# An encoder trunk on one core: the convolution's output product in three split passes, and the end of the token mixer in written order

## The chip, the core and the metric

The kernel runs on one core of a Trainium2 chip. Its time is the time of one execution on the device, in microseconds (us). A profile of one execution shows what each engine did: TensorE (PE, its weight loads PEld), VectorE (DVE), ScalarE (ACT), GpSimd (POOL), SyncE (SP, which issues most DMAs) and the DMA engines. All five run at the same time, each through its own instructions in order, and wait for each other by semaphores.

## What is computed

Two layers over 256 tokens of width 1024, in f32. Each layer is a SwiGLU block, a token mixer, a second SwiGLU block and a gated embedding. The change is in the mixer:

```
u = rms_norm(h)
q, k, v, c, g = split(u @ w_in)
y_attn = window_attention(q, k, v) @ w_attn_out
c_val, c_gate = split(c)
c = depthwise_conv(c_val * sigmoid(c_gate))        # 31 taps, 512 channels
c = silu(layer_norm(c))
y_conv = c @ w_conv_out                            # 512 -> 1024
g_attn, g_conv = split(sigmoid(g))
h = h + (g_attn * y_attn + g_conv * y_conv) @ w_o  # 1024 -> 1024
```

## The kernel before

Activations lie with channels on the 128 partitions and the 256 tokens along the free axis (T = 256), so a matmul has a weight block of 128 x 128 and a moving block of 128 x 256.

**Split products.** Most products are not done in f32. A weight and an activation are each split into a high and a low part of the type fp32r: ACT rounds the value to the high part (a CAST, L106 for weights), DVE subtracts it from the value for the low part (L107). The product is then three passes in TensorE, high x high, high x low, low x high (`mm3`, L322 to L330). Two products of the mixer are done in plain f32 on the raw weights: attn_out (tile `ps_ao`) and conv_out (`ps_co`), both in `products` at L892. The profile shows one plain f32 matmul as two passes.

**Weights.** The class `Weights` holds a list of loads (units, mostly 1 MB) and of prepared weights (specs). `get()` hands out the next weight and, before that, prepares weights up to `LOOK` = 6 ahead (less `rest`); `prep_upto` loads the raw unit into one of `RAW_BUFS` = 4 buffers (tile `raw`, DMAs at L80) and splits it. A raw buffer is free once its weights are split. `raw_spec` marks a weight that is used as it is: it is not split, and its raw buffer is held until TensorE has used it. `limit()` keeps loads from running past held buffers. `later(n, fn)` calls fn at the n-th next `get()`.

**Order.** A planner orders the instructions of each engine by the program's order, priorities and its own estimate of when things are ready. `keep_in_program_order` pins one instruction behind the one traced before it on its engine. `ws.lag` lowers the priority of weight splits. `group(products, evac)` runs a product and postpones the eviction of its result into the next group.

**The mixer's stages.** conv_in makes the convolution's input; its 31 taps a channel block run on DVE (L643) at low priority beside everything until the gates end. Attention: scores, softmax, `attend` (transposes `ps_pt`, copied by ACT to `pTs`), `gather` (`ps_o`). `gates` makes 16 blocks of g (`ps_g`); attention's steps for the second half of the tokens are hung between them by `later`. `squash` is the sigmoid of g on ACT. Then come four attn_out, with the layer norm between them: `ln_by_token` (transposes of y to `ps_yt`, statistics, `yn`) before the second, `ln_by_channel` (transposes back, `ps_yc`, silu on ACT) before the fourth. Then four conv_out; each eviction multiplies by the gate, adds the attention's part and splits the sum into `ym_h` and `ym_l` (L964, L965, `split` at L471). Then `mix_out` (`ps_wo`) with w_o, one double and six single, whose evictions add to x (L983) and split it for the next block.

PSUM has four tiles of one bank (`mm_tile`) and two of two banks (`at_tile`).

Of the kernel before, what the change touches and what calls it, by code (L numbers as in the profile page):

```python
# [31 lines left out]
NREL = 512  # L32
NEG = -1e9
LOOK = 6
RAW_BUFS = 4
BACKGROUND = 800
WEIGHTS_LAG = 100
ATTN = 7
# [7 lines left out]
class Weights:  # L46
# [4 lines left out]
    def __init__(self, tc, raw_pool, w_pool):  # L51
        self.tc, self.nc = tc, tc.nc
        self.raw_pool, self.w_pool = raw_pool, w_pool
        self.units, self.specs = [], []
        self.raw, self.ready, self.held, self.hooks = {}, {}, {}, []
        self.next_load = self.next_prep = self.next_get = 0
        self.rest, self.pin, self.lag, self.parts = 0, None, 0, 1

    def unit(self, k, n, sources):
# [61 lines left out]
    def later(self, n, fn):  # L121

        self.hooks.append((self.next_get + n - 1, fn))

    def finish(self):
        for _, fn in self.hooks:
            fn()
        self.hooks = []

    def get(self):  # L130
        i = self.next_get
        due = [fn for at, fn in self.hooks if at <= i]
        self.hooks = [h for h in self.hooks if h[0] > i]
        for fn in due:
            fn()
        p0 = self.tc.cur_priority
        self.tc.cur_priority = p0 + self.lag
# [7 lines left out]
def encoder_kernel(ctx: ExitStack, tc: tile.TileContext, a: dict, out: bass.AP):  # L145
# [105 lines left out]
    def mix_specs(l):  # L251
        w = a["w_in"][l]
        c0 = QD + 2 * P

        def conv_specs(j, n):
            uv = cols_unit(w, KD, c0 + j * P, n * P)
            ug = cols_unit(w, KD, c0 + CD + j * P, n * P)
            for c in range(n):
                ws.spec(KD, P, [(uv, 0, c * P, 0, P)])
                ws.spec(KD, P, [(ug, 0, c * P, 0, P)])  # L260

        conv_specs(0, 2)
        ukv = cols_unit(w, KD, QD, 256)
        for i in range(2):
            ws.spec(KC, 256, [(ukv, i * KC, 0, 0, 256)])
        for i in range(2):
            uq = cols_unit(w[i * KC * P : (i + 1) * KC * P], KC, 0, QD)
            for k in range(0, KC, 2):
                ws.spec(2, QD, [(uq, k, 0, 0, QD)])
        conv_specs(2, 2)  # L270
        g0 = QD + 2 * P + 2 * CD
        for j in range(8):
            u = cols_unit(w, KD, g0 + j * 256, 256)
            for c in range(2):
# [44 lines left out]
        return par[:, c0 + l * n + k : c0 + l * n + k + 1]  # L319


    def mm3(ps, w, x, first=True, last=True, k0=0, x_k0=0, n_k=None, cols=slice(0, P)):  # L322
        (wh, wl), (xh, xl) = w, x
        n_k = wh.shape[1] if n_k is None else n_k
        for k in range(n_k):
            kx = x_k0 + k
            f, e = first and k == 0, last and k == n_k - 1
            nc.tensor.matmul(ps, wh[:, k0 + k, cols], xh[:, kx, :], start=f, stop=False)  # L328
            nc.tensor.matmul(ps, wh[:, k0 + k, cols], xl[:, kx, :], start=False, stop=False)  # L329
            nc.tensor.matmul(ps, wl[:, k0 + k, cols], xh[:, kx, :], start=False, stop=e)  # L330

    def by_pass(ps, w, x, n_k):

# [136 lines left out]

    def split(dst, src, c=None):  # L471
        hi, lo = dst
        nc.scalar.copy(out=hi, in_=src)
        nc.vector.tensor_tensor(out=lo, in0=src, in1=hi.bitcast(F32), op=ALU.subtract)


    x_first = x_cur = new_x("xa", "x0")
# [146 lines left out]
    def mix(l, u, st, xn, stat):  # L624
        cw, kg, bias, sink = (late[n] for n in ("cw", "kg", "bias", "sink"))
        with tc.tile_pool(name="mix_pool", bufs=1) as mp:
# [4 lines left out]
            y = mp.tile([P, KC, T], F32, name="y")  # L631
            background = tc.cur_priority + BACKGROUND
            ws.lag = WEIGHTS_LAG

            def tap(i, t):
                src = cpad[:, i, t : t + T]
                w = cw[:, l, t, i : i + 1]
                if t == 0:
                    nc.vector.tensor_scalar(
                        out=y[:, i, :], in0=src, scalar1=w, scalar2=pcol("conv_b", l, i), op0=ALU.mult, op1=ALU.add  # L640
                    )
                else:
                    nc.vector.scalar_tensor_tensor(  # L643
                        out=y[:, i, :], in0=src, scalar=w, in1=y[:, i, :], op0=ALU.mult, op1=ALU.add
                    )

# [184 lines left out]
            def attend(qb, v):  # L831
                s = sc.pop((qb, v))
                ps = at_tile("ps_pt").rearrange("p (b c q) -> p b c q", b=2, c=GROUP)
                for c in reversed(range(GROUP)):
                    for b in range(2):
                        turned = nc.tensor.transpose(ps[:, b, c, :], s[:, c, b * P : (b + 1) * P], ident)
                        if (c, b) != (GROUP - 1, 0):
                            tc.keep_in_program_order(turned)
                pT = mp.tile([P, 2, GROUP * P], F32, name="pTs", tag="pTs", bufs=2)
                nc.scalar.copy(out=pT, in_=ps.rearrange("p b c q -> p b (c q)"))  # L840
# [2 lines left out]
            def gather(qb):  # L843
                pT = [sc.pop((qb, v)) for v in range(2)]
                ps = mm_tile("ps_o")
                for b in range(2):
                    for v in (1, 0):
# [5 lines left out]
                        if (b, v) != (0, 1):  # L853
                            tc.keep_in_program_order(mm)
                ov = ps.rearrange("p (c q) -> p c q", c=GROUP)
                nc.scalar.copy(out=o[:, :, qb * P : (qb + 1) * P], in_=ov[:, :, ::-1])
# [12 lines left out]
            def gates(i):  # L869
                ps, products = pair("ps_g", u, False)  # L870
# [4 lines left out]
                group(products, evac)  # L875
# [12 lines left out]
            def products(ps, x):  # L888
# [19 lines left out]
            def ln_by_token():  # L908
                mv = tmp.tile([P, 2, 2], F32, name="mv")
                ps = []  # L910
                for t in range(2):
                    ps.append(mm_tile("ps_yt"))
                    for i in range(KC):
                        nc.tensor.transpose(ps[t][:, i * P : (i + 1) * P], y[:, i, t * P : (t + 1) * P], ident)
                    six = tmp.tile([P, 6], F32, name="six")
                    nc.vector.bn_stats(out=six, in_=ps[t])
                    nc.vector.bn_aggr(out=mv[:, t, :], in_=six)
# [2 lines left out]
                nc.vector.reciprocal(out=rs, in_=rs)  # L920
                table(AF.Silu)
                for t in range(2):
                    nc.vector.tensor_scalar(
                        out=yn[:, t, :], in0=ps[t], scalar1=mv[:, t, 0:1], scalar2=rs[:, t : t + 1],
                        op0=ALU.subtract, op1=ALU.mult,
                    )

            def ln_by_channel():
                for i in range(0, KC, 2):
                    ps = mm_tile("ps_yc").rearrange("p (f t) -> p f t", f=2)  # L930
                    for f in range(2):
                        for t in range(2):
                            nc.tensor.transpose(
                                ps[:, f, t * P : (t + 1) * P], yn[:, t, (i + f) * P : (i + f + 1) * P], ident
                            )
                    for f in range(2):
                        nc.scalar.activation(
                            out=y[:, i + f, :], in_=ps[:, f, :], func=AF.Silu,
                            scale=pcol("conv_ln_g", l, i + f), bias=pcol("conv_ln_b", l, i + f),
                        )  # L940

            for i in range(KC):
# [14 lines left out]
            ]  # L957

            def conv_out(f):
                ps = mm_tile("ps_co")  # L960

                def evac():
                    gs = g[:, KD + f : KD + f + 2, :]
                    nc.vector.tensor_tensor(out=gs, in0=ps.rearrange("p (c t) -> p c t", c=2), in1=gs, op=ALU.mult)  # L964
                    nc.vector.tensor_tensor(out=gs, in0=gs, in1=g[:, f : f + 2, :], op=ALU.add)  # L965
                    yh, yl = ym[f // KC]
                    split((yh[:, f % KC : f % KC + 2, :], yl[:, f % KC : f % KC + 2, :]), gs)
# [7 lines left out]
            def mix_out(f, n):  # L975
# [10 lines left out]
                def some(c, w, k0, k1):  # L986
                    for i in range(2):
                        a0, a1 = max(k0, i * KC), min(k1, (i + 1) * KC)
                        if a0 < a1:
                            mm3(ps[c], w, ym[i], first=a0 == 0, last=a1 == KD, k0=a0, x_k0=a0 - i * KC, n_k=a1 - a0)  # L990

                def all_():
                    if n == 1:
# [138 lines left out]
```

## Time and profile before

| | us |
|---|---|
| median of 3 runs | 1102.88 (1102.76 to 1103.1) |
| the profiled execution | 1103.94 |
| its span, first to last instruction | 1102.1 |
| TensorE busy | 1089.4 |
| DVE busy | 810.6 |
| ACT busy | 610.2 |
| conv output product, each layer | 13.81 |

The span is shorter than the execution's time by what lies around the program. Durations are taken from the profiled execution. Matmuls overlap in the pipe, so TensorE's speed is read from one start to the next.

### The profile page before, as it was taken

What the parts mean: (1) busy time and instruction counts of PE and PEld (TensorE: products, weight loads), DVE (VectorE), ACT (ScalarE), POOL (GpSimd) and SP (SyncE); (2) the same over time, 40 slices, a digit from 0 to 9 for tenths busy, and PEclk for the clock granted to TensorE, in tenths of its full rate; (3) what the DMA queues carried; (4) which work ended last, traced back from release to release, by engine and by line L of the source; (5) the groups of instructions that cost most, each with busy time, mean ns of one, the idle gap of its engine ahead of it and who ended that gap; (6) DMA issues with size and microseconds to landing.
All of it is one profiled execution on the core that took longest, in us unless ns stands there. A gap on an engine that the chain in (4) does not pass through costs nothing.

```text
span 1102.1 us, 21871 instructions
## 1 busy us (share of the span) xinstructions
PE 1089.4 (99%) x9104; PEld 1063.0 (96%) x9104; DVE 810.6 (74%) x1217; ACT 610.2 (55%) x1028; POOL 86.6 (8%) x123
## 2 busy tenths in 40 slices
PE   8999999999999999999999999999999999999997
PEld 8999999999889999999999999999988999999997
DVE  5876666899868767666887666659996887776664
ACT  6654445676547555445764554457764665544452
POOL 2000001211002000001110000113100110000110
PEclk9999999999999999999999999999999999999999
DMA  8876546555075555556556564566432665554541
GB/s 269 274 248 216 182 169 219 178 189 154 4 260 192 196 199 195 179 173 226 189 187 208 175 213 153 175 229 198 144 116 84 232 230 190 192 194 156 188 154 39
DMA packets 195694, 202.99 MB, mean 184 GB/s; under 512 B 3731, under 2 KB 188899, under 8 KB 195596
## 3 DMA queue, kind: packets, MB, share of 16 engines
q1 hardware_dynamic: 195564, 201.60, 55.5%
q8 instruction: 71, 1.16, 0.4%
q14 instruction: 27, 0.22, 0.1%
q10 hardware_dynamic: 32, 0.01, 0.0%
HBM read 200.53 MB, written 1.06 MB: 183 GB/s over the span
## 4 chain that ended last, share of the span: by engine, by line
PE 94%; DVE 4%; DMA 1%; issue 1%; ACT 0%; POOL 0%; ACTq 0%; POOLq 0%
PE ps_gu L329 14%; PE ps_gu L330 14%; PE ps_gu L328 14%; PE ps_fo L328 7%; PE ps_fo L329 7%; PE ps_fo L330 7%; PE ps_g L328 3%; PE ps_g L330 3%; PE ps_g L329 3%; PE ps_co L892 3%; PE ps_ao L892 2%; DVE w_lo L107 2%; PE ps_c L328 1%; PE ps_pe L328 1%; PE ps_pe L329 1%; PE ps_pe L330 1%
## 5 line engine op out<-in xcount | busy, mean ns | idle before, releaser
L107 DVE TENSOR_TENSOR w_lo<-raw,w_hi 128x1024 fp32r<-128x1024 f32 (+2 forms) x369 | 441.4, 1200 | 212.1 <-ACT w_hi L106 212.0
L106 ACT CAST w_hi<-raw 128x1024 fp32r<-128x1024 f32 (+2 forms) x369 | 378.8, 1034 | 376.9 <-PE ps_gu L329 191.6
L329 PE MATMUL ps_fo<-h_lo,w_hi 128*128 128x256 f32 x704 | 193.0, 275 | 0.0
L330 PE MATMUL ps_fo<-h_hi,w_lo 128*128 128x256 f32 x704 | 193.0, 275 | 0.0
L328 PE MATMUL ps_fo<-h_hi,w_hi 128*128 128x256 f32 x704 | 193.0, 275 | 0.0
L329 PEld LDWEIGHTS ps_fo<-h_lo,w_hi 128*128 128x128 f32 x704 | 131.9, 188 | 0.0
L330 PEld LDWEIGHTS ps_fo<-h_hi,w_lo 128*128 128x128 f32 x704 | 131.9, 188 | 0.0
L328 PEld LDWEIGHTS ps_fo<-h_hi,w_hi 128*128 128x128 f32 x704 | 131.9, 188 | 0.0
L429 POOL TENSOR_TENSOR sq_acc<-sq_acc,sq 128x256 f32<-128x256 f32 x56 | 54.3, 969 | 840.9 <-ACT sq L428 840.4
L643 DVE SCALAR_TENSOR_TENSOR y<-cpad,cw,y 128x256 f32<-128x256 f32 x240 | 101.1, 476 | 0.2
L329 PE MATMUL ps_gu<-xf0l,w_hi 128*128 128x256 f32 x352 | 97.2, 276 | 0.1
L329 PE MATMUL ps_gu<-xf1l,w_hi 128*128 128x256 f32 x352 | 97.2, 276 | 0.1
L328 PE MATMUL ps_gu<-xn0h,w_hi 128*128 128x256 f32 x352 | 97.0, 276 | 0.0
L328 PE MATMUL ps_gu<-xf1h,w_hi 128*128 128x256 f32 x352 | 97.0, 275 | 0.0
L328 PE MATMUL ps_gu<-xf0h,w_hi 128*128 128x256 f32 x352 | 97.0, 275 | 0.0
L330 PE MATMUL ps_gu<-xf0h,w_lo 128*128 128x256 f32 x352 | 96.9, 275 | 0.0
L330 PE MATMUL ps_gu<-xf1h,w_lo 128*128 128x256 f32 x352 | 96.9, 275 | 0.0
L330 PE MATMUL ps_gu<-xn0h,w_lo 128*128 128x256 f32 x352 | 96.8, 275 | 0.0
L329 PE MATMUL ps_gu<-xn0l,w_hi 128*128 128x256 f32 x352 | 96.8, 275 | 0.0
L330 PE MATMUL ps_gu<-x0h,w_lo 128*128 128x256 f32 x338 | 93.3, 276 | 0.2 <-DVE w_lo L107 0.2
L328 PE MATMUL ps_gu<-x0h,w_hi 128*128 128x256 f32 x338 | 93.4, 276 | 0.0
L329 PE MATMUL ps_gu<-x0l,w_hi 128*128 128x256 f32 x338 | 93.0, 275 | 0.0
(233 smaller groups left out, 2654.2 us busy)
## 6 DMA issues: line engine op xcount, KB each, us to landing
raw<-in_w_ffn_in_dram SPq DMA_DIRECT2D x86, 1024.0 KB
raw<-in_w_in_dram SPq DMA_DIRECT2D x30, 1024.0 KB
raw<-in_w_ffn_out_dram SPq DMA_DIRECT2D x32, 896.0 KB
raw<-in_w_ffn_out_dram SPq DMA_DIRECT2D x16, 1024.0 KB
raw<-in_w_o_dram SPq DMA_DIRECT2D x8, 1024.0 KB
raw<-in_w_pe_gate_dram SPq DMA_DIRECT2D x8, 1024.0 KB
raw<-in_w_attn_out_dram SPq DMA_DIRECT2D x8, 512.0 KB
raw<-in_w_conv_out_dram SPq DMA_DIRECT2D x4, 1024.0 KB
```

The lines of the kernel that those rows point to most:

```text
L106: nc.scalar.copy(out=hv[:, at, d0 : d0 + w], in_=src),
L107: nc.vector.tensor_tensor(out=lv[:, at, d0 : d0 + w], in0=src, in1=hv[:, at, d0 : d0 + w].bitcast(F32), op=ALU.subtract,),
L328: nc.tensor.matmul(ps, wh[:, k0 + k, cols], xh[:, kx, :], start=f, stop=False)
L329: nc.tensor.matmul(ps, wh[:, k0 + k, cols], xl[:, kx, :], start=False, stop=False)
L330: nc.tensor.matmul(ps, wl[:, k0 + k, cols], xh[:, kx, :], start=False, stop=e)
L429: nc.gpsimd.tensor_tensor(out=self.acc, in0=self.acc, in1=sq, op=ALU.add)
L643: nc.vector.scalar_tensor_tensor(out=y[:, i, :], in0=src, scalar=w, in1=y[:, i, :], op0=ALU.mult, op1=ALU.add)
L892: nc.tensor.matmul(ps[:, c * T : (c + 1) * T], w[:, k, c * P : (c + 1) * P], x[:, k, :], start=k == 0, stop=k == KC - 1,)
```

## The change

conv_out takes split weights and a split y: its weights become ordinary specs (split by ACT and DVE, so their raw buffers come free one by one), `ln_by_channel` splits y into two new tiles `ys`, and `products3` runs the three passes, pinned. In the first conv_out the passes go one kind after the other over all blocks (so the low part of y is asked for last), and its result lies in an `at_tile`.

The order from the last gates on is written out: `last_gates` puts the second half's two `attend` and `gather` inside the last pair of gates, with the sigmoids behind the gather; the norm's transposes, silu and splits, the conv passes and all of mix_out's passes are pinned on their engines. `ln_by_token` moves to before the third attn_out. New is `ws.behind`: the weight splits of a `get()` are issued behind a given instruction of its engine (`issue_after`: order only), that is, behind the last tap, then behind yn, behind y's split, and behind the evictions of conv_out. `rest` is 2, 1 and 3 in this stretch, so that weights are prepared three ahead from the last attn_out on; three weights into the next block it is 0 again.

`RAW_BUFS` goes from 4 to 5; the 8 KB a partition for it come from a smaller scratch area for DMAs.

```diff
-RAW_BUFS = 4
+RAW_BUFS = 5
+DMA_SCRATCH = 8192
...
-        self.prep_upto(i + LOOK - self.rest)
+        with ExitStack() as queue:
+            for ins in self.behind:
+                queue.enter_context(self.tc.issue_after(ins))
+            self.prep_upto(i + LOOK - self.rest)
...
-                ws.raw_spec(u, KC, c * 256, 256)          # w_conv_out
+                ws.spec(KC, 256, [(u, 0, c * 256, 0, 256)])
...
-                (6, lambda: scores(1)), (7, lambda: gather(0)), (9, lambda: attend(1, 0)),
-                (10, lambda: attend(1, 1)), (12, lambda: gather(1)),
+                (6, lambda: scores(1)), (7, lambda: gather(0)),
...
+            def last_gates(i):
+                def products(ps):
...
+                    def first():
+                        some(0, 0, KC)
+                        for v in range(2):
+                            attend(1, v)
+                        some(0, KC, KD)
+                    def second():
+                        some(1, 0, 2)
+                        gather(1)
+                        some(1, 2, KD)
...
             for i in range(0, 2 * KD, 2):
-                gates(i)
-                if i == 12:
-                    for k in (0, 4, 8):
-                        squash(k)
+                if i == 2 * KD - 2:
+                    ws.behind = (last_tap[0].ins,)
+                    last_gates(i)
+                else:
+                    gates(i)
...
+                    parts = split(tuple(part[:, i : i + 2, :] for part in ys), y[:, i : i + 2, :])
+                    for ins in parts:
+                        tc.keep_in_program_order(ins)
+                return tuple(ins.ins for ins in parts)
 
             for i in range(KC):
-                if i == 1:
-                    ln_by_token()
+                if i == 0:
+                    ws.rest = 2
+                if i == 2:
+                    ws.rest, ws.behind = 1, ln_by_token()
                 if i == 3:
-                    ln_by_channel()
+                    ws.rest, ws.behind = 3, ln_by_channel()
...
-                group([lambda: products(ps, y)], evac)
+                def products3():
+                    (wh, wl), (yh, yl) = ws.get(), ys
+                    passes = ((wh, yh), (wl, yh), (wh, yl))
+                    if f == 0:
+                        steps = [(i, c, k) for i in range(3) for c in range(2) for k in range(KC)]
+                    else:
+                        steps = [(i, c, k) for c in range(2) for k in range(KC) for i in range(3)]
+                    for i, c, k in steps:
+                        wa, ya = passes[i]
+                        mm = nc.tensor.matmul(
+                            ps[:, c, :], wa[:, k, c * P : (c + 1) * P], ya[:, k, :],
+                            start=(i, k) == (0, 0), stop=(i, k) == (2, KC - 1),
+                        )
+                        tc.keep_in_program_order(mm)
...
+                    _, low = split((yh[:, f % KC : f % KC + 2, :], yl[:, f % KC : f % KC + 2, :]), gs)
+                    ws.behind = ((low if f == KD - 2 else added).ins,)
...
+            ws.behind = ()
+            ws.later(3, ws.catch_up)
```

More of the change, by code (lines that the diff above doesn't have):

```diff
@@ L56, in __init__ @@
         self.next_load = self.next_prep = self.next_get = 0
+        self.behind = ()
         self.rest, self.pin, self.lag, self.parts = 0, None, 0, 1
@@ L123, in later, with catch_up @@
         self.hooks.append((self.next_get + n - 1, fn))
+    def catch_up(self):
+        self.rest = 0
     def finish(self):
@@ L319, in pcol, with mm3 @@
         return par[:, c0 + l * n + k : c0 + l * n + k + 1]
-    def mm3(ps, w, x, first=True, last=True, k0=0, x_k0=0, n_k=None, cols=slice(0, P)):
+    def mm3(ps, w, x, first=True, last=True, k0=0, x_k0=0, n_k=None, cols=slice(0, P), pin=False):
         (wh, wl), (xh, xl) = w, x
@@ L327, in mm3 @@
             f, e = first and k == 0, last and k == n_k - 1
-            nc.tensor.matmul(ps, wh[:, k0 + k, cols], xh[:, kx, :], start=f, stop=False)
-            nc.tensor.matmul(ps, wh[:, k0 + k, cols], xl[:, kx, :], start=False, stop=False)
-            nc.tensor.matmul(ps, wl[:, k0 + k, cols], xh[:, kx, :], start=False, stop=e)
+            for wa, xa, a, b in ((wh, xh, f, False), (wh, xl, False, False), (wl, xh, False, e)):
+                mm = nc.tensor.matmul(ps, wa[:, k0 + k, cols], xa[:, kx, :], start=a, stop=b)
+                if pin:
+                    tc.keep_in_program_order(mm)
     def by_pass(ps, w, x, n_k):
@@ L472, in split @@
         hi, lo = dst
-        nc.scalar.copy(out=hi, in_=src)
-        nc.vector.tensor_tensor(out=lo, in0=src, in1=hi.bitcast(F32), op=ALU.subtract)
+        return (
+            nc.scalar.copy(out=hi, in_=src),
+            nc.vector.tensor_tensor(out=lo, in0=src, in1=hi.bitcast(F32), op=ALU.subtract),
+        )
     x_first = x_cur = new_x("xa", "x0")
@@ L633, in mix @@
             ws.lag = WEIGHTS_LAG
+            last_tap = [None]
             def tap(i, t):
@@ L642, in tap @@
                 else:
-                    nc.vector.scalar_tensor_tensor(
+                    last_tap[0] = nc.vector.scalar_tensor_tensor(
                         out=y[:, i, :], in0=src, scalar=w, in1=y[:, i, :], op0=ALU.mult, op1=ALU.add
@@ L836, in attend @@
                         turned = nc.tensor.transpose(ps[:, b, c, :], s[:, c, b * P : (b + 1) * P], ident)
-                        if (c, b) != (GROUP - 1, 0):
+                        if (c, b) != (GROUP - 1, 0) or qb == 1:
                             tc.keep_in_program_order(turned)
@@ L852, in gather @@
                         )
-                        if (b, v) != (0, 1):
+                        if (b, v) != (0, 1) or qb == 1:
                             tc.keep_in_program_order(mm)
                 ov = ps.rearrange("p (c q) -> p c q", c=GROUP)
-                nc.scalar.copy(out=o[:, :, qb * P : (qb + 1) * P], in_=ov[:, :, ::-1])
+                tc.keep_in_program_order(nc.scalar.copy(out=o[:, :, qb * P : (qb + 1) * P], in_=ov[:, :, ::-1]))
+                if qb == 1:
+                    for k in (0, 4, 8):
+                        squash(k)
             for at, fn in (
                 (0, lambda: scores(0)), (3, lambda: attend(0, 0)), (4, lambda: attend(0, 1)),
-                (6, lambda: scores(1)), (7, lambda: gather(0)), (9, lambda: attend(1, 0)),
-                (10, lambda: attend(1, 1)), (12, lambda: gather(1)),
+                (6, lambda: scores(1)), (7, lambda: gather(0)),
             ):
@@ L867, in mix, with gates, some @@
             g = mp.tile([P, 2 * KD, T], F32, name="g")
-            def gates(i):
-                ps, products = pair("ps_g", u, False)
+            def gates(i, products=None):
+                ps, whole_products = pair("ps_g", u, False)
                 def evac():
                     nc.vector.tensor_tensor(out=g[:, i : i + 2, :], in0=ps, in1=bcast(st.r, 2), op=ALU.mult)
-                group(products, evac)
+                group(products(ps) if products else whole_products, evac)
+            def last_gates(i):
+                def products(ps):
+                    w = []
+                    def some(c, k0, k1):
+                        if len(w) == c:
+                            w.append(ws.get())
+                        mm3(ps[:, c, :], w[c], u, first=k0 == 0, last=k1 == KD, k0=k0, x_k0=k0, n_k=k1 - k0, pin=True)
+                    def first():
[7 more added lines that the diff above has]
+                        some(1, 2, KD)
+                    return [first, second]
+                gates(i, products)
             def squash(i):
@@ L913, in ln_by_token @@
                     for i in range(KC):
-                        nc.tensor.transpose(ps[t][:, i * P : (i + 1) * P], y[:, i, t * P : (t + 1) * P], ident)
+                        turned = nc.tensor.transpose(ps[t][:, i * P : (i + 1) * P], y[:, i, t * P : (t + 1) * P], ident)
+                        tc.keep_in_program_order(turned)
                     six = tmp.tile([P, 6], F32, name="six")
@@ L922, in ln_by_token @@
                 for t in range(2):
-                    nc.vector.tensor_scalar(
+                    normed = nc.vector.tensor_scalar(
                         out=yn[:, t, :], in0=ps[t], scalar1=mv[:, t, 0:1], scalar2=rs[:, t : t + 1],
@@ L926, in ln_by_token @@
                     )
+                return (normed.ins,)
+            ys = tuple(rows(mp, KC, "y_" + part) for part in "hl")
             def ln_by_channel():
@@ L932, in ln_by_channel @@
                         for t in range(2):
-                            nc.tensor.transpose(
+                            turned = nc.tensor.transpose(
                                 ps[:, f, t * P : (t + 1) * P], yn[:, t, (i + f) * P : (i + f + 1) * P], ident
                             )
+                            tc.keep_in_program_order(turned)
                     for f in range(2):
-                        nc.scalar.activation(
+                        act = nc.scalar.activation(
                             out=y[:, i + f, :], in_=ps[:, f, :], func=AF.Silu,
@@ L940, in ln_by_channel @@
                         )
+                        tc.keep_in_program_order(act)
+                    parts = split(tuple(part[:, i : i + 2, :] for part in ys), y[:, i : i + 2, :])
+                    for ins in parts:
+                        tc.keep_in_program_order(ins)
+                return tuple(ins.ins for ins in parts)
             for i in range(KC):
-                if i == 1:
-                    ln_by_token()
+                if i == 0:
+                    ws.rest = 2
+                if i == 2:
+                    ws.rest, ws.behind = 1, ln_by_token()
                 if i == 3:
-                    ln_by_channel()
+                    ws.rest, ws.behind = 3, ln_by_channel()
                 attn_out(2 * i)
@@ L959, in conv_out @@
             def conv_out(f):
-                ps = mm_tile("ps_co")
+                if f == 0:
+                    ps = at_tile("ps_co").rearrange("p (c t) -> p c t", c=2)[:, :, :T]
+                else:
+                    ps = mm_tile("ps_co").rearrange("p (c t) -> p c t", c=2)
                 def evac():
                     gs = g[:, KD + f : KD + f + 2, :]
-                    nc.vector.tensor_tensor(out=gs, in0=ps.rearrange("p (c t) -> p c t", c=2), in1=gs, op=ALU.mult)
-                    nc.vector.tensor_tensor(out=gs, in0=gs, in1=g[:, f : f + 2, :], op=ALU.add)
+                    nc.vector.tensor_tensor(out=gs, in0=ps, in1=gs, op=ALU.mult)
+                    added = nc.vector.tensor_tensor(out=gs, in0=gs, in1=g[:, f : f + 2, :], op=ALU.add)
                     yh, yl = ym[f // KC]
-                    split((yh[:, f % KC : f % KC + 2, :], yl[:, f % KC : f % KC + 2, :]), gs)
-                group([lambda: products(ps, y)], evac)
+                    _, low = split((yh[:, f % KC : f % KC + 2, :], yl[:, f % KC : f % KC + 2, :]), gs)
[3 more added lines that the diff above has]
+                    passes = ((wh, yh), (wl, yh), (wh, yl))
+                    if f == 0:
+                        steps = [(i, c, k) for i in range(3) for c in range(2) for k in range(KC)]
+                    else:
+                        steps = [(i, c, k) for c in range(2) for k in range(KC) for i in range(3)]
[4 more added lines that the diff above has]
+                            start=(i, k) == (0, 0), stop=(i, k) == (2, KC - 1),
+                        )
+                        tc.keep_in_program_order(mm)
+                group([products3], evac)
             for f in range(0, KD, 2):
@@ L989, in some @@
                         if a0 < a1:
-                            mm3(ps[c], w, ym[i], first=a0 == 0, last=a1 == KD, k0=a0, x_k0=a0 - i * KC, n_k=a1 - a0)
+                            mm3(
+                                ps[c], w, ym[i], first=a0 == 0, last=a1 == KD, k0=a0, x_k0=a0 - i * KC, n_k=a1 - a0,
+                                pin=True,
+                            )
                 def all_():
@@ L1119 @@
     from concourse.bass_utils import run_bass_kernel_spmd as run
-    nc = bacc.Bacc("TRN2", target_bir_lowering=False, num_devices=1)
+    nc = bacc.Bacc("TRN2", target_bir_lowering=False, num_devices=1, dynamic_dma_scratch_size=DMA_SCRATCH)
     arrays, args = {}, {}
```

## The prediction

> **What bounds the kernel now.** I read the busy table first, then the waits on TensorE, then the chain that ended last, then the timelines of the mixer's end.
>
> ```profile
> PE 1089.4 (99%) x9104; PEld 1063.0 (96%) x9104; DVE 810.6 (74%) x1217; ACT 610.2 (55%) x1028; POOL 86.6 (8%) x123
> PEclk9999999999999999999999999999999999999999
> ...
> PE ps_o L848 <- ACT pTs L840: 2.2, 2, 1.1
> PE ps_stat L438 <- POOL sq_acc L429: 1.2, 1, 1.2
> PE ps_yc L933 <- DVE yn L923: 0.4, 2, 0.2
> ```
>
> TensorE works through 99% of the span at the full granted clock, and its listed waits come to a few microseconds. So time leaves this kernel in two ways only: TensorE gets less to do, or one of those waits goes. The other engines matter where they make TensorE wait.
>
> ```profile
> 309.94 13.81 PE ps_co L892 x64
> 849.67 13.81 PE ps_co L892 x64
> ...
> 289.50 0.28 PE L328 MATMUL ps_g<-xm0h,w_hi 128*128 128x256 f32 x1
> ...
> 293.47 0.28 PE L330 MATMUL ps_g<-xm0h,w_lo 128*128 128x256 f32 x1
> ```
>
> The first two rows are the whole conv output product, once per layer: 64 passes in 13.81 us, 0.2158 us each. The source has 32 plain f32 products per layer, so each is two passes, 0.4316 us. The last two rows are a run of split products, 36 of them, 35 steps in 3.97 us: 0.1134 us from one start to the next (the 0.28 us of one is its latency in the pipe). Three of them make one product, 0.3402 us.
>
> **The conv product (conv_out, products3).** It takes away 64 passes a layer and adds 32 x 3 = 96. That is 96 x 0.1134 = 10.89 us against 13.81 us, 2.92 us less per layer, 5.84 us in both. TensorE has no spare time there, so this lies on the path. Bounds on the pitch: the best is 0.1134, since no run here is faster; the worst is that of the old pass, 0.2158, which would cost 6.9 us a layer. I take 0.1134, because the new passes have the shape of the rows quoted and weights that change each time, as there. [...]
>
> **The gather (last_gates).** Now:
>
> ```profile
> 283.98 1.03 PE L836 MATMUL ps_pt<-ident,s 128*128 128x128 f32 x8
> 286.12 1.94 PE L848 MATMUL ps_o<-pTs,vt 128*64 128x512 f32 x8 [1.10 <-ACT pTs L840]
> ...
> 285.05 1.01 ACT L840 COPY pTs<-ps_pt 128x1024 f32<-128x1024 f32 x1 [0.44 <-PE ps_pt L836]
> ...
> 318.51 1.99 ACT L106 CAST w_hi<-raw 128x1024 fp32r<-128x1024 f32 x2 [1.90 <-DMA raw<-in_w_o_dram]
> ```
>
> The second copy out of the transposes ends at 286.06 and the eight gather products wait 1.10 us for it, with 48 gate products (two weights of 24) queued behind. The written order puts 12 + 6 = 18 gate products, 2.04 us, between the last transpose and the gather; the copies need about 1.1 us after it. The wait should go: 2.2 us over both layers. Bounds: 0, if the weights' casts that now also run on ACT (1.0 us each, last row) stand ahead of the copy, and 2.2. The sigmoids (squash) follow the gather's copy, and the evictions of attn_out need them only later.
>
> **The added splits.** Four casts (ACT) and four subtractions (DVE) of conv weights a layer, and two pairs for y:
>
> ```profile
> 302.00:306.00 4.00, 3.78 (x20) 2.88 (x19) 3.60 (x9) 1.58 (x2) 0.00 (x0) 1.00 0.74 262
> 306.00:310.00 4.00, 4.00 (x23) 3.56 (x22) 2.54 (x4) 3.82 (x6) 0.00 (x0) 1.00 0.00 0
> 310.00:317.00 7.00, 7.00 (x34) 6.17 (x33) 1.97 (x3) 2.00 (x2) 0.00 (x0) 1.00 0.86 298
> 317.00:324.00 7.00, 7.00 (x36) 6.20 (x35) 6.67 (x9) 3.78 (x5) 0.00 (x0) 1.00 0.89 296
> 324.00:332.00 8.00, 8.00 (x72) 8.00 (x72) 5.18 (x8) 2.10 (x4) 0.00 (x0) 1.00 0.80 267
> 332.00:340.00 8.00, 8.00 (x73) 8.00 (x72) 7.71 (x11) 7.25 (x13) 3.05 (x3) 1.00 0.41 136
> ...
> 317.44 1.21 DVE L107 TENSOR_TENSOR w_lo<-raw,w_hi 128x1024 fp32r<-128x1024 f32 x1
> 318.57 0.68 DVE L965 TENSOR_TENSOR g<-g 128x512 f32<-128x512 f32 x1
> ...
> 322.46 0.68 DVE L474 TENSOR_TENSOR ym_l<-g,ym_h 128x512 fp32r<-128x512 f32 x1
> 323.06 0.68 DVE L965 TENSOR_TENSOR g<-g 128x512 f32<-128x512 f32 x1
> ...
> 320.40 0.61 ACT L473 CAST ym_h<-g 128x512 fp32r<-128x512 f32 x1
> ```
>
> In the window rows the third figure after the length is DVE, the fourth ACT. From start to start a weight's subtraction takes 1.13 us and a 512-column step 0.60. DVE gets 4 x 1.13 + 2 x 0.60 = 5.7 us a layer, ACT 4 x 1.0 + 2 x 0.6 = 5.2. From 302 to 332 DVE is busy 19.96 of 30 us, so it has 10.0 us free, and ACT 16.7; less the 2.9 us by which the stretch shortens, 7.1 and 13.8. The work fits and is hidden, if its order lets it: cost 0. If that cover is gone, it costs up to 5.7 us a layer (below).
>
> DVE in the conv product: each conv_out now needs product, sum and low half, 3 x 0.60, and one w_o subtraction, 1.13: 2.93 us, against 24 x 0.1134 = 2.72 us on TensorE. I walked this from the end of the first conv_out: DVE loses 0.21 us per step and has the last low half some 2.65 us after the last conv product (0.60 + 0.60 + cast 0.61 + 0.60 and the lag). mix_out(0, 2) first runs 2 x 18 = 36 products, 4.08 us, that do not need it. Margin 1.4 us, so cost 0. Its w_lo are looked ahead by three weights instead of six, 8.2 us of products: a split (1.0 on ACT, 1.13 on DVE) stays ahead. From 332 on DVE has 7.71 of 8 us busy, but that is looking ahead for the next stage; one step there needs 1.13 and two short steps against 2.72.
>
> **The written order of the normalization.**
>
> ```profile
> 294.39 2.43 DVE L643 SCALAR_TENSOR_TENSOR y<-cpad,cw,y 128x256 f32<-128x256 f32 x5
> ...
> 301.95 1.28 DVE L916 BATCH_NORM_STATS2 six<-ps_yt 128x6 f32<-128x512 f32 x2
> 303.16 0.30 DVE L917 BATCH_NORM_AGGREGATE mv<-six 128x2 f32<-128x6 f32 x2
> 303.82 0.17 DVE L920 RECIPROCAL rs<-rs 128x2 f32<-128x2 f32 x1 [0.36 <-ACT rs L919]
> 304.02 1.53 DVE L923 TENSOR_SCALAR yn<-ps_yt,mv,rs 128x512 f32<-128x512 f32 x2
> ...
> 306.48 3.46 PE ps_ao L892 x16
> ```
>
> The taps end at 296.8, behind them come two conv weights' subtractions (2.3 us) and one eviction (0.6): DVE is free at 299.7, about when the transposes of y, now behind two whole attn_out, are done. From the first statistics to the end of yn 301.95 to 305.55 passes, 3.6 us, of which a first part overlaps the transposes; one attn_out, 3.46 us, covers it. That is the cover of today, where the wait is 0.2 us a layer. I take -0.2 over both layers, bounds -0.4, both waits of the row, and +1.2 (one eviction of 0.60 in each chain). The silu, cast and low half of y stand under the last attn_out.
>
> **The fifth raw buffer and smaller edits.** Buffers free a load one unit earlier. Inside the kernel no TensorE wait names a load, so nothing; at the start one does, by way of ACT:
>
> ```profile
> 19.77 1.05 ACT L106 CAST w_hi<-raw 128x1024 fp32r<-128x1024 f32 x1 [1.63 <-DMA raw<-in_w_ffn_in_dram]
> ...
> 10.00:15.00 5.00, 4.82 (x42) 4.63 (x41) 4.60 (x8) 4.68 (x10) 1.23 (x2) 1.00 0.93 269
> 15.00:20.00 5.00, 4.79 (x43) 4.60 (x42) 1.61 (x2) 2.01 (x4) 3.15 (x4) 1.00 1.00 306
> ```
>
> Behind that cast stand the last two squares, then the sum on POOL, then ps_stat, which TensorE waits 1.2 us for. The load was issued when a buffer came free, and would go earlier; but the DMA share is already 0.93 and 1.00, so little comes of it. Bounds 0 and -1.2; I take -0.4, a third. The parameters' loads stand behind one more megabyte on SP's queue (3.4 us at the 306 GB/s of the row above); nothing is near enough to wait. The w_o loads go up in SP's queue, the smaller scratch moves addresses only: 0. For waits of the written order that I can't place I add 0.4 (bounds 0 and 4, the first rival).
>
> **Sum.** -5.84 - 2.2 - 0.2 - 0.4 + 0.4 = -8.24 us. The profiled execution took 1103.94 us (span 1102.1); it goes to 1095.7. The median, 1102.88, stands 1.06 below it and goes to 1094.6.
>
> **Rivals.**
> 1. The order gives part of it back: the 0.21 us a step that DVE loses adds up over four conv_out (0.84 us a layer) and comes out as a wait, and the chain silu, cast, low half (1.1 us beyond the silu) is not covered by the last attn_out. About 1.9 us a layer: 1094.6 + 3.9 = 1098.5. For it: DVE's 2.93 against 2.72. Against: the 1.4 us margin and the 7.1 us free.
> 2. Slower. DVE runs in order, and the conv weights' subtractions, now behind the last tap, push everything after them; TensorE, pinned, has no other product to take. If all 5.7 us of a layer come out as waits, 2 x 5.7 = 11.4: 1094.6 - 0.4 + 11.4 = 1105.6. It decides from waits of 4.3 us a layer on, where they eat 8.6. [...] Against: DVE's free time.
> 3. The gather's wait only moves, to another spot of the new order, as ACT does casts there: 1096.8.
> 4. The product doesn't get faster: a pitch of 0.144 would make 96 passes cost 13.8 us, and leave 1094.6 + 5.8 = 1100.4. Against: no split product of this shape in the rows has such a pitch.
>
> **Chances.** Forecast 0.70 (alone 1092.5 to 1096.8), first rival 0.13, second 0.09, third 0.05, fourth 0.03. About 0.2%, 2.2 us, can be told from no change here. Slower is the second rival less what of it ends near zero, 0.08; same 0.03; the rest faster, 0.89. The range reaches from 1092.5 (5.84 + 2.2 + 0.4 + 1.2 = 9.64 off gives 1093.2, and 0.7 for what a wait's row may leave out at its restart) to 1099.0, past the first rival; what is left out is the second, the fourth and a rest.
>
> **What would show it.** Right: the conv product takes 10.9 us a layer in 96 passes; no wait of ps_o for pTs; waits of ps_wo and ps_co on TensorE below 0.5 us a layer; ps_stat at the start waits under 1.2 us. Wrong: a pitch above 0.12 in ps_co; ps_wo waiting for ym or w_lo by over 1 us; ps_yc waiting for yn by more than 0.5 us; split products elsewhere, in ps_gu and ps_fo, off 0.1134, which would be the moved addresses.

## The result, and the profile after

The changed kernel takes 1095.6 us (median of 4 runs, 1095.11 to 1098.71) against 1102.96 (the kernel before, with a fourth run added to the three above): ratio 0.9936, 95% interval 0.9925 to 0.9948. The forecast was 1094.6, in a range of 1092.5 to 1099.0. Beside other kernels on another chip it took 1098.52 against 1103.21 (0.9950, 0.9937 to 0.9963). The profiled execution took 1098.71 us with a span of 1096.9; it is some 3 us longer than the other three, of which no trace was kept.

First the busy table and the waits on TensorE:

```profile
PE 1083.9 (99%) x9168; PEld 1062.1 (97%) x9168; DVE 824.1 (75%) x1229; ACT 621.7 (57%) x1040; POOL 86.7 (8%) x123
...
PE ps_stat L447 <- POOL sq_acc L438: 3.4, 1, 3.4
...
PE ps_yc L977 <- DVE yn L964: 0.5, 2, 0.3
```

64 matmul passes more, 5.5 us less work on TensorE. The gather's wait for pTs is gone, there are no ps_co or ps_wo waits, and ps_stat at the start waits 3.4 us where it waited 1.2. Then the chain that ended last, in order of time (start, length):

```profile
288.41 1.75 PE ps_pt L848 x16
290.16 2.05 PE ps_g L337 x18
292.21 1.89 PE ps_o L860 x8
...
301.03 0.48 DVE y L655
301.52 2.27 DVE w_lo L109 x2
...
304.39 1.20 DVE six L957 x2
...
306.37 1.54 DVE yn L964 x2
...
308.94 3.46 PE ps_ao L932 x16
312.39 10.92 PE ps_co L1035 x96
...
847.57 10.96 PE ps_co L1035 x96
```

The order is as written: all transposes, 18 gate products, the gather with nothing between; two conv weights' w_lo right behind the last tap; 96 conv passes in 10.92 and 10.96 us, where 64 took 13.81.

By the starts on TensorE the mixer, from conv_in's first product to the next block's first, takes 146.91 and 146.95 us; before it was 151.09 and 150.96. Another 0.4 us a layer goes in the first 43 products of the next block (5.30 us before, 4.88 after). The rest of the kernel, beyond the start, is the same to 0.1 us. So the mixers and what follows them directly give 9.0 us, and the start takes some back: 3.8 us in the profiled execution, some 1.7 by the medians.

### The profile page after: what moved, and what is told of

Read it like the earlier page. It is cut to its first block, busy times and chain, and to the rows that moved or that the text cites. A ratio compares the mean times of both kernels' runs of the same rounds, so it can differ in the third digit from the quotient of the medians.

```text
span 1096.9 us, 22021 instructions
## 1 busy us (share of the span) xinstructions
PE 1083.9 (99%) x9168; PEld 1062.1 (97%) x9168; DVE 824.1 (75%) x1229; ACT 621.7 (57%) x1040; POOL 86.7 (8%) x123
## 4 chain that ended last, share of the span: by engine, by line
PE 95%; DVE 2%; ACT 2%; DMA 1%; POOL 0%; issue 0%; ACTq 0%; POOLq 0%
PE ps_gu L337 43%; PE ps_fo L337 22%; PE ps_g L337 8%; PE ps_c L337 4%; PE ps_pe L337 4%; PE ps_wo L337 4%; PE ps_co L1035 2%; PE ps_pp L337 1%; PE ps_s L804 1%; DMA raw<-in_w_ffn_in_dram 1%; ACT g L918 1%; PE ps_o L860 1%; PE ps_q L764 1%; PE ps_q L765 1%; PE ps_q L763 1%; PE ps_pt L848 1%
## 5 line engine op out<-in xcount | busy, mean ns | idle before, releaser
L109 DVE TENSOR_TENSOR w_lo<-raw,w_hi 128x1024 fp32r<-128x1024 f32 (+2 forms) x377 | 450.7, 1201 | 200.0 <-ACT w_hi L108 199.6
L108 ACT CAST w_hi<-raw 128x1024 fp32r<-128x1024 f32 (+2 forms) x377 | 387.9, 1034 | 371.9 <-PE ps_gu L337 199.7
```

The source lines that it names most:

```text
L108: nc.scalar.copy(out=hv[:, at, d0 : d0 + w], in_=src),
L109: nc.vector.tensor_tensor(out=lv[:, at, d0 : d0 + w], in0=src, in1=hv[:, at, d0 : d0 + w].bitcast(F32), op=ALU.subtract,),
```

## The experiments

"Four buffers" below means the changed kernel with `RAW_BUFS = 4` and the old scratch. "Mixer" is the stretch named above, in both layers; "taps" is the time from the first gate product to the end of the last tap, first layer. The last two columns are of the one profiled execution, the others of all runs.

| kernel | median, us | before, same chip | ratio (95%) | mixers, us | taps, us |
|---|---|---|---|---|---|
| before | | | | 151.1, 151.0 | 62.4 |
| changed, again (e13) | 1098.52 | 1103.21 | 0.9950 (0.9937 to 0.9963) | 146.9, 146.9 | 63.3 |
| four buffers (e1) | 1094.04 | 1103.70 | 0.9913 (0.9898 to 0.9929) | 147.0, 147.0 | 63.3 |
| fifth buffer alone (e2) | 1121.12 | 1103.70 | 1.0159 (1.0144 to 1.0174) | 160.7, 160.8 | 70.2 |
| split alone (e3) | 1129.45 | 1103.70 | 1.0234 (1.0219 to 1.0249) | 157.9, 159.4 | 71.3 |
| squares first (e4) | 1096.65 | 1103.70 | 0.9939 (0.9926 to 0.9951) | 146.9, 146.9 | 63.3 |
| order only (e5) | 1099.90 | 1103.32 | 0.9970 (0.9958 to 0.9982) | 149.8, 149.3 | 63.3 |
| old gather (e6) | 1097.95 | 1103.32 | 0.9945 (0.9933 to 0.9958) | 148.2, 148.2 | 61.4 |
| no release (e8) | 1114.75 | 1103.32 | 1.0105 (1.0091 to 1.0119) | 157.3, 157.5 | 72.6 |
| split and tap (e10) | 1120.62 | 1103.32 | 1.0151 (1.0138 to 1.0165) | 152.8, 158.6 | 61.9 |
| release, no pins (e9) | 1094.05 | 1103.21 | 0.9917 (0.9904 to 0.9930) | 147.1, 147.1 | 62.3 |
| no tap release (e11) | 1094.10 | 1103.21 | 0.9916 (0.9903 to 0.9929) | 146.6, 146.8 | 65.2 |
| squares first, four buffers (e12) | 1094.02 | 1103.21 | 0.9916 (0.9903 to 0.9928) | 146.9, 147.0 | 63.3 |

Outside the mixers and the start only e3 and e10 lose much: the next block's first 43 products take 10.3 and 10.3 us in e3, 10.1 and 8.8 in e10, and 5.3 before.

**Four buffers: where the start's loss comes from**

```diff
-RAW_BUFS = 5
-DMA_SCRATCH = 8192
+RAW_BUFS = 4
...                  (the scratch has its old size again)
```

> The changed kernel with four raw buffers and the larger DMA scratch, as before the change. Theory (order at the start): with the fifth buffer the planner puts three casts, which wait for a load, ahead of the last square on ACT, and the first ps_stat waits 3.4 us instead of 1.2; with four buffers the order is the old one, that wait is 1.2 again, the mixers keep their gain of 4.6 + 4.4 = 9.0 us: 1103.0 - 9.0 = 1094.0. Rival (the mixer needs the fifth buffer): the start is as before, but a w_o or conv weight comes late in both mixers and TensorE waits 1 us or more in each: 1096 or more.

1094.04, as the theory said, and the mixers keep all of their gain. One part of the theory missed: ps_stat doesn't wait at all here, where it waited 1.2 us before the change. The order on ACT is the old one, but the second cast doesn't wait for its load. The start, on ACT, from the timelines: the changed kernel first, then this one.

```profile
17.28 1.99 ACT L108 CAST w_hi<-raw 128x1024 fp32r<-128x1024 f32 x2
19.18 0.41 ACT L437 ACTIVATE sq<-x 128x256 f32<-128x256 f32 x1
20.75 2.94 ACT L108 CAST w_hi<-raw 128x1024 fp32r<-128x1024 f32 x3 [1.17 <-DMA raw<-in_w_ffn_in_dram]
23.60 0.41 ACT L437 ACTIVATE sq<-x 128x256 f32<-128x256 f32 x1
```

```profile
17.09 1.99 ACT L107 CAST w_hi<-raw 128x1024 fp32r<-128x1024 f32 x2
18.99 0.71 ACT L436 ACTIVATE sq<-x 128x256 f32<-128x256 f32 x2
21.98 3.90 ACT L107 CAST w_hi<-raw 128x1024 fp32r<-128x1024 f32 x4 [2.27 <-DMA raw<-in_w_ffn_in_dram]
```

With five buffers the planner puts three casts, the first of them waiting for its load, between the last two squares; the last square, which the first norm's sum needs, starts at 23.60. With four it stands ahead of them, and ends by 19.70.

**The changed kernel again**

> The changed kernel as it is, five buffers, beside the others on one chip. Theory (the fifth buffer costs at the start alone): the mixers take 146.9 us each, ps_stat waits about 3 us, 1 to 3 us more than with four buffers: 1095 to 1097. Rival (the first profile's wait was chance): no wait of ps_stat over 1.2 us and 1094.

The wait is no chance: 3.3 us again. The time, 1098.52, is above what the theory gave. Two of the six runs take 1095.18 and 1095.69 us and four 1098.35 to 1100.0, as above three took 1095.1 to 1095.6 and one 1098.71; both profiles are of the longer kind. What the shorter executions lack, no trace shows. The runs of e11 and e12 on the same chip lie between 1093.01 and 1094.66. By medians the changed kernel takes 4.5 us more than e12, which differs from it by the squares too, and 1.6 us more than e1, which ran on another chip.

**Squares first, with five and with four buffers**

```diff
     r_cur = stat.finish(5)
+    ws.behind = (stat.last.ins,)
+    ws.later(8, lambda: setattr(ws, "behind", ()))
...                  (stat.last is the last square; e12 has four buffers besides)
```

> The changed kernel, five buffers, with the first weights' casts issued on ACT behind the last square of the start (order only), so that the first norm doesn't stand behind a load. Theory (order at the start): ps_stat doesn't wait, or under 0.3 us; against four buffers another 1.2 us: 1094.0 - 1.2 = 1092.8. Rival (the loads at the start are late by themselves): the wait moves to the next gate and up products, 1095.6.

> The changed kernel with four raw buffers and the first casts behind the last square. Theory (with four buffers the parameters' loads are as early as before, and the first ps_stat doesn't wait): no wait of ps_stat, none over 0.5 us in ps_cw or ps_rb, 1093 to 1094, that is as fast as four buffers alone or up to 1 us faster. Rival (at the start everything hangs on the loads): the wait comes out elsewhere, 1094 to 1096.

The ps_stat wait goes in both. With five buffers the time does not fall as the theory said: 1096.65, where it gave 1092.8. The rival is nearer in time, but the wait comes out in another place than it named. The waits on TensorE of e4:

```profile
PE ps_cw L561 <- ACT par L220: 1.7, 1, 1.7
...
PE ps_rb L573 <- ACT cw L562: 1.6, 1, 1.6
```

These are the tables made from the late parameters, whose loads stand on SP behind nine loads of weights instead of eight with four buffers. The changed kernel's own trace has no such wait: the parameters are as late there (their copy starts at 45.3 us, against 45.9 in e4 and 43.6 in e1), but TensorE, held up before, asks for them later. So at the start the loss has two causes, the place of the squares and the place of the parameters, of which the first hides the second. With four buffers ps_cw and ps_rb wait 0.2 us at most, and the edit gives nothing over e1, as the theory allowed.

**The fifth buffer alone**

```diff
-RAW_BUFS = 4
+RAW_BUFS = 5
+DMA_SCRATCH = 8192
...                  (the smaller scratch, as in the change)
```

> The kernel before with the fifth raw buffer and the smaller scratch alone. Theory (order at the start): ps_stat waits about 3.4 us instead of 1.2 and nothing else moves, the mixers take 151.5 us as before: 1103.0 + 1.7 to 1103.0 + 3.8, so 1104.7 to 1106.8. Rival (earlier loads help, as forecast, and the loss at the start of the changed kernel comes from elsewhere): 1102.6, ps_stat waiting under 1.2.

Both theories fell: it is 17.4 us slower by the medians, and in the profiled execution the mixers alone take 9.6 and 9.9 us more. Its waits on TensorE; the w_lo subtractions on DVE from 275 to 295 us (length, busy us and count), before and here; and ACT between the two copies out of the transposes:

```profile
PE ps_yc L934 <- DVE yn L924: 6.1, 2, 3.1
PE ps_o L849 <- ACT pTs L841: 5.9, 2, 3.0
```

```profile
275.00:295.00 20.00, 0.00 (x0) 1.00 0.00 1
```

```profile
275.00:295.00 20.00, 4.82 (x4) 0.91 0.30 100
```

```profile
286.77 1.99 ACT L107 CAST w_hi<-raw 128x1024 fp32r<-128x1024 f32 x2 [0.23 <-DMA raw<-in_w_o_dram]
288.67 1.00 ACT L841 COPY pTs<-ps_pt 128x1024 f32<-128x1024 f32 x1
```

Before, all four raw buffers were held by the unsplit attn_out and conv_out weights through this stretch, so nothing could be loaded or split, and DVE had it for the taps. That hold was a brake. A fifth buffer lets w_o units in one after the other: SP issues the first at 269.5 us, where it was 301.3 before. This does two things. On ACT two casts stand between the copies, the gather waits 3.0 us, and altogether attn_out starts 4.7 us later after the first gate. On DVE the splits stand ahead of taps, the last tap ends 7.8 us later after the first gate, and the norm comes late: attn_out and conv_out together take 4.9 us more. The granted clock is 0.91 in the mean from 275 to 295 us, where it was 1.00 before (the rows from 275 to 295 above; more of that in the next run).

**The split alone**

```diff
-                ws.raw_spec(u, KC, c * 256, 256)
+                ws.spec(KC, 256, [(u, 0, c * 256, 0, 256)])
...
+                    split(tuple(part[:, i : i + 2, :] for part in ys), y[:, i : i + 2, :])
...
-                group([lambda: products(ps, y)], evac)
+                group([products3], evac)
```

> The kernel before with the split conv product alone: weights split, y split, three passes, four buffers, and the planner's order everywhere. Theory (less work on TensorE is the main term and DVE and ACT have room): -2.6 us a layer, 1103.0 - 5.2 = 1097.8, the gather's wait of 1.1 us stays. Rival (without the written order the added splits make TensorE wait): waits of 1 us or more in ps_co, ps_ao or ps_wo in each layer, 1100 to 1103.

The theory fell, and the rival had the sign but not the size: it is 25.8 us slower. The conv product itself is as fast as in the changed kernel (11.04 us from its first start to mix_out's), but splitting its weights takes the same brake off.

```profile
275.00:295.00 20.00, 6.03 (x5) 1.00 0.32 106
```

```profile
303.18 2.04 DVE L643 SCALAR_TENSOR_TENSOR y<-cpad,cw,y 128x256 f32<-128x256 f32 x4
```

```profile
PE ps_yc L935 <- DVE yn L923: 6.5, 2, 3.2
PE ps_co L977 <- ACT y_h L473: 4.4, 2, 2.2
PE ps_o L848 <- ACT pTs L840: 3.3, 2, 1.7
PE ps_gu L329 <- DVE xf0l L462: 2.6, 2, 1.7
```

The taps end at 305.2, behind the evictions of two attn_out. The mixers lose 6.8 and 8.5 us; another 5.0 us a layer goes at the start of the next block, whose first products wait for the low part of their input (the last row above): on DVE, w_lo splits stand ahead of it there too.

And the long wait costs twice here. The windows around the wait for yn (length, TensorE busy with its count; the granted clock is the third figure from the end):

```profile
306.00:310.00 4.00, 0.77 (x7) 0.56 (x6) 3.57 (x8) 1.58 (x2) 0.00 (x0) 0.99 0.24 83
310.00:313.00 3.00, 3.00 (x9) 2.37 (x9) 0.23 (x1) 0.00 (x0) 0.00 (x0) 0.50 0.00 0
313.00:316.00 3.00, 2.86 (x16) 2.29 (x14) 0.69 (x1) 0.42 (x1) 0.00 (x0) 0.95 0.00 0
```

After 3.2 us of waiting the granted clock is 0.50 through the 3.00 us of the second row; with the 0.99 and 0.95 beside it that makes some 3.4 us at half clock (an estimate). By it attn_out's passes stand 0.43 us apart there instead of 0.2158 (an estimate, 0.2158 / 0.50). Shorter waits had it too: here it also fell, to 0.71, behind two waits of 1.7 and 0.9 us in the next block, and in e10, the next run, to 0.66 behind one of 2.3 us (first row e3, second e10). In the changed kernel's start it comes with the 3.4 us wait (third and fourth row), and the split passes show what it does: those from 27.21 to 28.49 us start 0.21 us apart, those from 28.89 to 29.95 us, at the full clock again, 0.12.

```profile
356.00:360.00 4.00, 2.98 (x15) 2.73 (x15) 3.63 (x6) 2.10 (x3) 1.13 (x1) 0.71 0.42 141
```

```profile
300.00:305.00 5.00, 4.10 (x11) 3.34 (x12) 3.75 (x8) 3.03 (x3) 0.00 (x0) 0.66 1.06 373
```

```profile
20.00:25.00 5.00, 2.53 (x23) 2.33 (x21) 3.94 (x4) 4.20 (x5) 2.23 (x2) 1.00 1.08 384
25.00:30.00 5.00, 4.03 (x21) 3.85 (x22) 4.43 (x5) 3.75 (x4) 0.92 (x1) 0.66 0.42 145
```

**One release added to the split**

```diff
+                if i == 2 * KD - 2:
+                    ws.behind = (last_tap[0].ins,)
                 gates(i)
...
                 if i == 3:
+                    ws.behind = ()
                     ln_by_channel()
```

> The kernel before with the split conv product and one release: the weight splits of the last two gates and of the first three attn_out are issued on DVE behind the last tap; planner's order otherwise, four buffers. Theory (the displaced taps are the cause of the loss of the split alone): most of the 26 us comes back and the saved passes show: 1103 - 5 + up to 3 for splits that now come late, 1098 to 1101. Rival (the loss has many causes, the pins are needed too): 1110 or more.

The rival came out. The taps end early, at 61.9, yet it is 17.3 us slower. From DVE's timeline and the waits:

```profile
295.62 4.63 DVE L108 TENSOR_TENSOR w_lo<-raw,w_hi 128x1024 fp32r<-128x1024 f32 x4
300.16 0.68 DVE L878 TENSOR_TENSOR g<-ps_g,r_x 128x512 f32<-128x512 f32 x1
```

```profile
PE ps_yc L942 <- DVE yn L930: 3.5, 1, 3.5
PE ps_gu L333 <- DVE xf0l L466: 2.9, 1, 2.9
PE ps_gu L333 <- DVE xf1l L466: 2.6, 2, 1.7
PE ps_ao L899 <- DVE g L878: 2.3, 1, 2.3
```

The four splits that were held come out in one block behind the last tap, ahead of the gates' and attn_out's evictions, and later ones ahead of mix_out's and of the next block's input. So one release is not enough; that the splits have to be let out a few at a time is what the next runs bear out.

**No release, pins kept**

```diff
-                    ws.rest, ws.behind = 1, ln_by_token()
+                    ln_by_token()
...                  (all settings of rest and behind, alike)
```

> The changed kernel with four raw buffers and all pins, but without the releases: no splits held behind the last tap, yn, y or the evictions, and six weights ahead throughout. Theory (splits that may run early stand ahead of taps on DVE, as in the split alone): the last tap ends 8 us later, the yn wait grows to 3 us or more and TensorE, pinned, waits 6 us or more in each layer: 1106 to 1112. Rival (the written order alone holds the splits back): 1094 to 1096.

The theory held, and the loss is larger than it gave: 1114.75, 20.7 us over four buffers. The taps end at 72.6, 9.3 us later, and TensorE waits for y, before it can wait for yn:

```profile
PE ps_yt L952 <- DVE y L654: 13.6, 4, 5.3
```

The written order on TensorE alone does not hold DVE's splits back: from 275 to 295 us DVE has 6.12 us of w_lo, where four buffers have none.

**No tap release, and releases without pins**

```diff
-                    ws.behind = (last_tap[0].ins,)
```

> The changed kernel with four raw buffers, without the one release behind the last tap; the later releases, the limit of splits ahead and the pins stay. Theory (what counts is how many splits are let in ahead; here it is two a layer, 2.3 us on DVE, and the last tap has 1.6 us to spare before the transposes of y): 0.7 us a layer, 1094 to 1096. Rival (any split ahead of the last tap goes straight to TensorE): 2.3 us or more a layer, 1098.6 or more.

```diff
-                        tc.keep_in_program_order(mm)
...                  (all pins new in the change, alike; last_gates stays)
```

> The changed kernel with four raw buffers and all releases and three-ahead splits, but none of the new pins: TensorE and ACT go as the planner orders them, from the last gates to the end of mix_out. Theory (it is the releases on DVE that keep the mixer's end whole, the pins only fix the gather): at most the gather's wait comes back, 1094 to 1097. Rival (the pins are needed as much): waits of 2 us or more in each layer, 1099 or more.

Both theories held: 1094.10 and 1094.05 are no different from four buffers. Without the tap release two more splits go in ahead of the last tap, which is 1.9 us later, and that fits under the first two attn_out. Without the pins the gather gives 0.7 us a layer back, as a wait of attn_out (below), and mix_out's start gains some.

```profile
PE ps_ao L931 <- ACT o L867: 1.4, 2, 0.7
```

**Order only, and the old gather**

```diff
-                ws.spec(KC, 256, [(u, 0, c * 256, 0, 256)])
+                ws.raw_spec(u, KC, c * 256, 256)
...                  (y is not split, plain f32 passes, and no release behind y's split)
```

> The changed kernel with four raw buffers and the conv product in plain f32 on raw weights, as before the change; the written order and the releases stay. Theory (the split saves passes and nothing else, the written order saves the gather's wait and part of the norm's): the mixers lose the 2.5 us that conv_out took less, and take 149.4 us each: 1094.0 + 5 = 1099. Rival (the split also helps by freeing raw buffers early): w_o comes late as it did before, TensorE waits in ps_wo, and it is 1101 or more.

```diff
+                (9, lambda: attend(1, 0)), (10, lambda: attend(1, 1)), (12, lambda: gather(1)),
...
-                    last_gates(i)
+                    gates(i)
```

> The changed kernel with four raw buffers, but with the second half's attend and gather hung between the gates by the old hooks, not written into the last pair. Theory (the gather's wait is worth what the profile of before showed): ps_o waits 1.1 us for pTs in each layer again, from the gates to attn_out 59.2 us instead of 58.0: 1094.0 + 2.5 = 1096.5. Rival (with the conv casts now on ACT at that place the copies come later): 2 us or more a layer, 1098 or more.

In the mixers both theories held, and they price the parts. Without the split the mixers take 149.8 and 149.3 and the time is 1099.90: the split is worth 2.8 and 2.3 us, the order with the releases 1.3 and 1.7. With the old gather they take 148.2, 1.2 us more each (1.6 up to attn_out, of which 0.4 comes back behind it), and the old wait is back:

```profile
PE ps_o L859 <- ACT pTs L851: 2.2, 2, 1.1
```

Its time, 1097.95, is 1.4 us further off than these 2.5 us; that part lies at the start and stays open.

## Why the prediction was right, and where it was not

The time came out 1.0 us above the forecast. The conv product and the gather, which make up nearly all of the forecast, came as forecast. Two errors of the rest, 1.2 us too little taken off in the mixers and the next block and 2.0 us too much at the start, partly cancel; that the number is this close is in part luck. Both layers together, in us; the products by the ends of the passes on TensorE, as in the rows of the chain:

| | forecast | measured |
|---|---|---|
| conv product | -5.84 | -5.74 |
| first gate product to attn_out (the gather) | -2.2 | -2.4 |
| attn_out with the norm | -0.2 | -0.3 |
| mix_out (forecast: waits that could not be placed) | +0.4 | +0.3 |
| first 43 products of the next block | | -0.85 |
| start (the fifth buffer) | -0.4 | +1.6 to +1.7 by medians |

- **The conv product**: 10.89 us a layer forecast, 10.92 and 10.96 measured. The pitch held, 0.1138 and 0.1142 us a pass (10.92 and 10.96 over 96), so the fourth rival did not come.
- **The gather**: the wait is gone and no other took its place, so the third rival did not come. It is worth 1.2 us a layer, where the row of the wait had 1.10; where the other 0.1 us lies was not taken apart.
- **The added splits, cost 0**: right for the kernel as changed. There are no ps_wo or ps_co waits, so the first rival did not come. But the condition attached to it, "if its order lets it", carried the result. The price named for the case that the cover is gone, 5.7 us a layer, was too low: it counted DVE's added work alone. Without the releases (e8) the mixers take 10.3 and 10.6 us more, since the splits also push out taps, and the waits behind them come with a granted clock of 0.68 from 305 to 310 us and 0.64 from 310 to 315. The second rival had the right mechanism, as e10 shows: an eviction of the gates starts on DVE at 300.16 us, behind 4.63 us of splits. In the kernel as changed the releases keep it away.
- **The norm and the waits that could not be placed**: near their forecasts, -0.3 and +0.3. No wait of the written order is listed; mix_out is 0.3 us longer in both layers together.
- **The next block**: its first products lost 0.85 us less in both layers. The forecast had no term for it, and no run takes it apart. It is most of the first error.
- **The fifth buffer, -0.4**: the failed step. The prediction asked only when the loads land, and took the order of the other engines as given. With the fifth buffer the order on ACT at the start is another, and ps_stat, which was to wait under 1.2 us, waits 3.4: +1.6 us against e1, +4.5 beside e12. "The parameters' loads ... nothing is near enough to wait" was wrong too: e4 shows 1.7 and 1.6 us. And "inside the kernel ... nothing" holds in the changed kernel, whose mixers take 146.9 us with five buffers and 147.0 with four; in the kernel before, without the releases and the pins, the buffer costs 17.4.

The version that beats both kernels is the change with four buffers, 1094.04, ratio 0.9913 to the kernel before.

What stays open: which of rest and the later settings of behind does the work in e8, as they were taken away together; the spread of a few us at the start, which the kernel before has as well; and what of the fifth buffer's cost belongs to the smaller DMA scratch, which went with it in every run. The order of casts and splits, which the traces show, speaks for the buffer, but no run has the one without the other.

## What to carry to other kernels

A buffer that is held too long can be a brake that the schedule depends on: before freeing it or adding another, ask what will run ahead in the time won, and which engine's last due work it displaces. Where weights are prepared ahead on an engine that also has work on the path, limit how many may be let in and let them out a few at a time; a single ordering edge moves the whole block to behind itself (e10, four splits in 4.63 us). Test the parts of a combined change alone: here two of them, the fifth buffer and the split, lose 17 and 26 us by themselves, and a third, the releases, makes the split a gain.

## What the runs showed of the hardware

The gather's wait of 1.1 us on TensorE cost 1.2 a layer (e6 against e1). These long waits of TensorE came with a lower granted clock: 0.50 for 3.00 us behind 3.2 us (e3), 0.66 from 25 to 30 us with the 3.4 us wait (the changed kernel), 0.91 from 275 to 295 us with 3.0 us (e2), 0.68 and 0.64 in the two stretches of 5 us from 305 us on, with waits of up to 5.3 us (e8). 3.4 us at 0.50 are 1.7 us of work more (an estimate). These runs show no one length from which it sets in: the clock also fell behind a wait of 2.3 us (0.66, e10), behind 1.7 and 0.9 us close together (0.71, e3) and behind 0.8 and 1.3 us at the changed kernel's start (0.77 from 9 to 15 us). It was 1.00 behind a wait of 2.2 us (ps_co in e3, 315 to 330 us), and behind the 1.1 us waits of the gather before (286 to 294 us and 822 to 834 us). A split f32 product, three passes of 0.1134 us, takes 79% of the plain one, two passes of 0.2158 (the kernel before).
